# Four gate tiles ahead of the convolution's fourth tile in a two-layer hybrid diffusion step

## The chip, the cores and the metric

The kernel runs on one core of one Trainium2 chip. The metric is the device time of one execution in microseconds (us), from which a median over runs is taken. PE stands for TensorE, DVE for VectorE, ACT for ScalarE, POOL for GpSimd and SP for SyncE, whose queue issues the transfers. A line number such as L1300 is a line of the kernel before; in the changed kernel the same code stands two lines lower from L576 on.

## The reference

A step of a small diffusion backbone runs two layers over 128 context tokens and 1,024 latent tokens of width 1,024. All arithmetic is float32. In each layer a token's row is normalised and modulated to h, one projection of h gives the inputs of three branches, and the branches are gated, projected and added to the residual:

```python
(shift, scale, gate) = SiLU(cond) @ W_ada + b_ada
h = RMSNorm(x) * (1 + scale) + shift
[A | B | C] = split(h @ W_in)
y_A = B_g * conv3(C_g * x_A) * SiLU(g_A)
y_B = neighbourhood_attention(q, k, v) * SiLU(g_B)
y_C = RMSNorm(bidirectional_gated_linear_attention(q, k, v)) * SiLU(g_C)
merged = sum_b sigmoid(h @ W_gate + b_gate)_b * (y_b @ W_branch[b])
x = x + gate * (merged @ W_out)
```

Branch A is a convolution of three taps along the tokens. Branch B lets every latent token attend to a window of the 16 x 64 grid and to all cached context keys. Branch C carries a 64 x 128 state per head through the sequence in both directions, chunk by chunk.

## The kernel before, in words

**Precision and tiles.** Each float32 operand of the large products is held as a high and a low part, and a product is three matmuls (high by high, high by low, low by high). The 1,152 tokens stand in three chunks of 384. A feature tile is 128 columns of a weight matrix: `load_w` (L186) lets SP fetch it (512 KB into the tile `wraw`), ACT make the high part `whi` (L182) and POOL the low part `wlo` (L183). `mode_a` (L223) multiplies it by one chunk: 8 x 3 = 24 matmuls of 128 x 384 into one bank `ps`, of which there are two in turn. Whatever reads a `ps` bank must be done before PE may fill it again, two chunks later.

**The main work of a layer** is written out in `layer` (L527). After the projections of values, keys and queries come four convolution tiles (`conv`, L1275), four tiles of SiLU for the attention (`silus`, L1326), sixteen gate tiles (`gates`, L589), four gated tiles of the linear attention (`gated`, L1317) and five more gate tiles. They all multiply h, so on PE they look alike; they differ in what empties the banks:

- `conv` makes four products per chunk and tile. In its first half ACT copies `xa` (L1285) and DVE multiplies `u` (L1288). Over the whole row of 1,154 columns DVE then forms the three taps `cv` (L1291 to L1293). In the second half DVE multiplies by the taps into `y1` (L1300; the profile calls the tile `y`), and ACT, DVE and POOL form the SiLU `th` (L1307 to L1309).
- `gates` makes one product per chunk. ACT alone empties the bank (L596), and SP stores `gt` to `gd` (L597).
- `silus` empties the bank with ACT (L1332) and DVE (L1333).

**The side work** is woven into PE's order by the class `Pace`: each main matmul adds its planned microseconds to a credit, and when that is full, one step of the side work is written into PE's order. The side work is first the linear attention (`gla`) and then the neighbourhood attention (`attention`). The places where it goes therefore depend on how many main matmuls have been written, not on which tile they belong to. In `gla` the recurrence of states (L1160) is a chain of DVE operations that is written after the last chunk's matmuls:

```python
nS = g1.tile([128, GH, DV], F32, name="gs", tag=("qk1", "la")[i % 2])
...
for h in range(GH):
    dve.scalar_tensor_tensor(nS[r, h], S[r, h], dec[r, c + 1, h:h + 1], u[:, h], op0=ALU.mult, op1=ALU.add)
```

It has 56 such operations in each layer. In `attention` every item (a head, a row group and a column block) has a stage with scores (DVE L933, ACT L934, DVE L938 and L939), one with transposes (ACT L962, DVE L963) and one that multiplies by the values.

**A third strand** is `adaln` (L281), the modulation for the gate and the next layer. It is a list of generators called `extras`; `silus`, `gates` and `gated` call `extra()` after each chunk, and every other call makes one step of it. A step fetches 512 KB of `w_ada` into a `wraw` tile and multiplies it on ACT (L294), DVE (L299) and POOL (L296, L297).

**What sets the order.** PE's instructions keep the order in which the program writes them. The order on DVE, ACT, POOL and SP is chosen by the scheduler that builds the program, so operations can move ahead of others that were written earlier. Each engine then runs its own list strictly in order.

Of the kernel before, what the change touches and what calls it, by code (L numbers as in the profile page):

```python
# [112 lines left out]
def hybrid_step(ctx: ExitStack, tc: tile.TileContext, io: dict):  # L113
# [4 lines left out]
    def pool(name, bufs=2, side="left", **kw):  # L118
        return tc.tile_pool(name=name, bufs=bufs, side=side, reuse_waits="tile", **kw)
# [66 lines left out]
    def load_w(pieces, nk, lo_engine=gps):  # L186
        return split_w(*raw_w(pieces, nk), lo_engine)

    def wview(w, l, c0, n):
        return w[l].rearrange("(k p) c -> p k c", p=128)[:, :, c0:c0 + n]  # L190
# [336 lines left out]
    def layer(l):  # L527
        d = Scratch(l)
        win = lambda c0, n: wview(io["w_in"], l, c0, n)
        fw_stack = ExitStack()  # L530
        fw = fw_stack.enter_context(pool(f"fw_{l}"))
        s1_stack = ExitStack()
        with ExitStack() as s0_stack:
            projections(l, d, win, s1_stack, s0_stack, fw)
        main_us = 47.0 + (16 + 4 + 4 + 21) * 3 * 24 * 0.163 + (19.0 if l + 1 < DEPTH else 8.0)
        extras = []

        turn = [0]

        def extra():  # L540
            turn[0] += 1
            while extras and turn[0] % 2:
                try:
                    next(extras[0])
                    return
                except StopIteration:
                    extras.pop(0)

        def side():
            yield from gla(l, d)  # L550
            left = main0 + main_us - pace.main
            pace.rate = NH * 23 / max(left - 20.0, 40.0)
            yield from attention(l, d)

        main0 = pace.main

        def begin():
            s1_stack.close()
            pace.start(side(), RATE_G)

        pace.defer(14.0, begin)
        with pool(f"vp_{l}") as vp:
            values(l, d, win, vp)
        cv_stack = ExitStack()
        cvp = cv_stack.enter_context(pool(f"cv_{l}"))
        extras = [adaln(l, 2, cvp, wraw)]
        if l + 1 < DEPTH:
            extras += [adaln(l + 1, 0, cvp, wraw), adaln(l + 1, 1, cvp, wraw)]
        for m in range(4):
            conv(l, m, win, fw, cvp, d.yd[0])  # L570
        for m in range(4):
            silus(l, m, win, fw, GN, d.yd[1], extra)
        gates(l, range(0, 16), fw, "y1", 2, d.gd, extra)
        for m in range(4):
            gated(l, m, win, fw, GG, d.ogd, keep(d.yd[2]), extra)
        gates(l, range(16, 21), fw, "y1", 2, d.gd, extra)  # L576
        while extras:
            turn[0] = 0
            extra()
        pace.drain()  # L580
        cv_stack.close()
        fw_stack.close()
        with pool(f"yp_{l}", 3) as yp:
            first = branch_input(l, d, 0, yp, yp)
            gates(l, range(21, 24), yp, "gl", 3, d.gd)
            rest = branches(l, d, yp, first)
        output(l, *rest)

    def gates(l, tiles, tp, tag, bufs, gd, extra=lambda: None):  # L589

        for m in tiles:
            wg = load_w([wview(io["w_gate"], l, m * 128, 128)], KD)
            for c in range(NCH):
                ps = mode_a(wg, H, KD, c)
                gt = tp.tile([128, CH], F32, name="gt", tag=tag, bufs=bufs)
                act.activation(gt, ps, ACTF.Tanh, scale=0.5, bias=C["b_gate"][:, l, m:m + 1])  # L596
                sp.dma_start(gd[m * 128:(m + 1) * 128, c * CH:(c + 1) * CH], gt)  # L597
                extra()
# [23 lines left out]
    def values(l, d, win, vp):  # L622

        for u in range(2):
            mode_b([win(VN + u * 256, 256)], H, split_values(l, d, vp, u))
        for j in range(4):
            a = d.vd[TP + KCS[j]:TP + KCS[j] + 1, :]
            src = bass.AP(tensor=a.tensor, offset=a.offset, ap=[[128 * BW, 16], [1, 64 * BW]])
            sp.dma_start(d.vw[j], src)
# [641 lines left out]
    def segs(c):  # L1271

        return ((0, 128, 0), (128, 256, 130)) if c == 0 else ((0, 384, CH * c + 2),)

    def conv(l, m, win, fw, cvp, yd):  # L1275
        wx = load_w([win(XA + m * 128, 128)], KD)
        wc = load_w([win(CA + m * 128, 128)], KD)
        u = cvp.tile([128, T + 4], F32, name="u", tag="u", bufs=1)
        gps.memset(u[:, 0:1], 0.0)
        gps.memset(u[:, 129:131], 0.0)  # L1280
        gps.memset(u[:, T + 3:T + 4], 0.0)
        for c in range(NCH):
            ps = mode_a(wx, H, KD, c)
            xa = cvp.tile([128, CH], F32, name="xa", tag="xa")
            act.copy(xa, ps)  # L1285
            ps = mode_a(wc, H, KD, c)
            for o, n, p in segs(c):
                dve.tensor_tensor(u[:, p + 1:p + 1 + n], ps[:, o:o + n], xa[:, o:o + n], op=ALU.mult)  # L1288
        cv = cvp.tile([128, T + 2], F32, name="cv", tag="cv", bufs=1)
        w = lambda i: C["conv_w"][:, l, m, i:i + 1]  # L1290
        dve.tensor_scalar(cv, u[:, 0:T + 2], w(0), None, op0=ALU.mult)  # L1291
        dve.scalar_tensor_tensor(cv, u[:, 1:T + 3], w(1), cv, op0=ALU.mult, op1=ALU.add)
        dve.scalar_tensor_tensor(cv, u[:, 2:T + 4], w(2), cv, op0=ALU.mult, op1=ALU.add)  # L1293
        wb = load_w([win(BA + m * 128, 128)], KD)
        wg = load_w([win(GA + m * 128, 128)], KD)
        for c in range(NCH):
            ps = mode_a(wb, H, KD, c)
            y1 = fw.tile([128, CH], F32, name="y1", tag="y1")
            for o, n, p in segs(c):
                dve.tensor_tensor(y1[:, o:o + n], ps[:, o:o + n], cv[:, p:p + n], op=ALU.mult)  # L1300
            ps = mode_a(wg, H, KD, c)
            keep(yd)(c, m, silu2_times(ps, y1, fw, "th"))
# [9 lines left out]
    def keep(yd):  # L1312
        def f(c, m, y):
            sp.dma_start(yd[m * 128:(m + 1) * 128, c * CH:(c + 1) * CH], y)
        return f

    def gated(l, m, win, fw, c0, od, out, extra):  # L1317
        wg = load_w([win(c0 + m * 128, 128)], KD)
        for c in range(NCH):
            y1 = fw.tile([128, CH], F32, name="y1", tag="y1")  # L1320
            sp.dma_start(y1, od[m * 128:(m + 1) * 128, c * CH:(c + 1) * CH])
            ps = mode_a(wg, H, KD, c)
            out(c, m, silu2_times(ps, y1, fw, "th"))
            extra()

    def silus(l, m, win, fw, c0, zd, extra):  # L1326

        wg = load_w([win(c0 + m * 128, 128)], KD)
        for c in range(NCH):
            ps = mode_a(wg, H, KD, c)  # L1330
            th = fw.tile([128, CH], F32, name="th", tag="th")
            act.activation(th, ps, ACTF.Tanh, scale=0.5)  # L1332
            dve.scalar_tensor_tensor(th, th, 1.0, ps, op0=ALU.add, op1=ALU.mult)  # L1333
            keep(zd)(c, m, th)
            extra()

    def branch_input(l, d, b, yp, home):

        Y = {}
        for c in range(NCH):  # L1340
            if home is yp:
                Y[c] = [yp.tile([128, 4, CH], F32R, name=f"y{x}", tag=f"y{x}", bufs=3) for x in "hl"]
            else:
                Y[c] = [hp.tile([128, KD, CH], F32R, name=f"h{x}", tag=f"h{x}") for x in ("hi", "lo")]
            yh, yl = Y[c]
            at = lambda t, k: t[k * 128:(k + 1) * 128, c * CH:(c + 1) * CH]
            for k in range(4):
                ys = yp.tile([128, CH], F32, name="ys", tag="ys", bufs=4)
                sp.dma_start(ys, at(d.yd[b], k))
                if b == 1:  # L1350
                    on = yp.tile([128, CH], F32, name="on", tag="ys", bufs=4)
                    sp.dma_start(on, at(d.ond, k))
                    gps.tensor_tensor(ys, ys, on, op=ALU.mult)
                act.copy(yh[:, k], ys)
                dve.tensor_tensor(yl[:, k], ys, yh[:, k].bitcast(F32), op=ALU.subtract)
        return Y
# [102 lines left out]
    with tc.manual_schedule(engines={mybir.EngineType.PE}):  # L1459
        for l in range(DEPTH):  # L1460
            layer(l)
# [93 lines left out]
```

## Time and profile before

| | |
|---|---|
| median of 3 runs | 2787.06 us (2779.57 to 2788.96) |
| profiled execution, its own time | 2782.12 us |
| its span | 2780.3 us |
| PE busy | 2705.2 us, 97% of the span |
| DVE busy | 1189.2 us, 43% |
| ACT busy | 936.9 us, 34% |
| POOL busy | 1042.1 us, 37% |
| mean granted clock of PE | 0.996 |

The span runs from the first instruction's start to the last one's end; the execution's own time is 1.8 us longer. PE's matmuls overlap, so its busy share tells when it had something to do and not that it ran at its peak. A wait in the trace is a stretch in which an engine had nothing to run, with the instruction of another engine (the releaser) that ended it. Layer 0's main work with its side work fills about 350 to 1120 us of the span, layer 1's about 1720 to 2490 us.

### The profile page before, as it was taken

The numbers are of one execution on the slowest core, as the hardware profiler recorded it, in microseconds if no ns is written. First come the engines' busy times: TensorE is split into PE (matmuls) and PEld (weight loads), VectorE is DVE, ScalarE is ACT, GpSimd is POOL, SyncE is SP. The second block draws the span as 40 slices with busy tenths as digits, with TensorE's granted clock in tenths as the row PEclk, the third lists the DMA queues.
The fourth block names the chain that finished last, engine by engine and source line by source line (L and its number), as shares of the span: only waits on it lengthen the run. The fifth ranks groups of instructions, "written<-read, shape, count | busy, mean of one in ns | idle before, by whom it ended". The sixth has DMA issues, their size and how long they took to land. (4 is left out here: it accounts for less than half of the span.)

```text
span 2780.3 us, 47973 instructions
## 1 busy us (share of the span) xinstructions
PE 2705.2 (97%) x18548; PEld 2655.0 (95%) x18548; DVE 1189.2 (43%) x2400; ACT 936.9 (34%) x1802; POOL 1042.1 (37%) x884
## 2 busy tenths in 40 slices
PE   6999999999999999999989999999999999999999
PEld 4999999999999999999989999989999999999999
DVE  5344335545444443335173452364453334432441
ACT  5243322233444433312242442222244343342120
POOL 0343233463574431167343332333532112212852
PEclk9999999999999999999999999999999999999999
DMA  7444672365565653565234447623655455435651
GB/s 235 120 130 129 196 238 71 110 183 142 168 181 154 169 157 94 177 185 181 74 122 119 127 127 226 211 68 124 164 147 154 134 146 154 137 111 180 176 181 69
DMA packets 455740, 415.26 MB, mean 149 GB/s; under 512 B 84740, under 2 KB 422028, under 8 KB 455248
## 3 DMA queue, kind: packets, MB, share of 16 engines
q1 hardware_dynamic: 455504, 412.13, 50.1%
q8 instruction: 146, 2.39, 0.4%
q14 instruction: 90, 0.74, 0.1%
HBM read 292.04 MB, written 136.74 MB: 154 GB/s over the span
## 5 line engine op out<-in xcount | busy, mean ns | idle before, releaser
L131 PE MATMUL ps<-hhi,whi 128*128 128x384 f32 x2368 | 807.3, 341 | 17.6 <-DVE y L1300 6.7
L131 PE MATMUL ps<-hhi,wlo 128*128 128x384 f32 x2368 | 804.9, 340 | 0.3
L131 PE MATMUL ps<-hlo,whi 128*128 128x384 f32 x2368 | 805.1, 340 | 0.0
L183 POOL TENSOR_TENSOR wlo<-wraw,whi 128x1024 fp32r<-128x1024 f32 (+2 forms) x172 | 369.0, 2145 | 803.1 <-ACT whi L182 739.9
L131 PE MATMUL ps<-whi,hhi 128*128 128x256 f32 (+1 forms) x1984 | 567.1, 286 | 5.8 <-DVE ro L616 2.4
L131 PE MATMUL ps<-wlo,hhi 128*128 128x256 f32 (+1 forms) x1984 | 567.0, 286 | 2.1 <-DVE wlo L183 2.1
L131 PE MATMUL ps<-whi,hlo 128*128 128x256 f32 (+1 forms) x1984 | 566.6, 286 | 0.0
L131 PEld LDWEIGHTS ps<-hhi,whi 128*128 128x128 f32 x2368 | 447.0, 189 | 23.7 <-DVE y L1300 6.5
L131 PEld LDWEIGHTS ps<-hlo,whi 128*128 128x128 f32 x2368 | 447.1, 189 | 2.1 <-issue 1.4
L131 PEld LDWEIGHTS ps<-hhi,wlo 128*128 128x128 f32 x2368 | 446.8, 189 | 1.8 <-issue 0.9
L131 PEld LDWEIGHTS ps<-whi,hhi 128*128 128x128 f32 x1984 | 379.9, 192 | 9.3 <-PE ps L131 3.1
L131 PEld LDWEIGHTS ps<-wlo,hhi 128*128 128x128 f32 x1984 | 379.9, 191 | 4.3 <-DVE wlo L183 3.3
L131 PEld LDWEIGHTS ps<-whi,hlo 128*128 128x128 f32 x1984 | 380.1, 192 | 0.6 <-issue 0.3
L182 ACT CAST whi<-wraw 128x1024 fp32r<-128x1024 f32 (+1 forms) x200 | 189.4, 948 | 372.0 <-PE ps L131 164.2
L963 DVE TENSOR_TENSOR ptl<-psb,pth 128x640 fp32r<-128x640 f32 x128 | 105.3, 823 | 189.2 <-ACT pth L962 188.9
L934 ACT ACTIVATE prob<-prob,mn 128x640 f32<-128x640 f32 x128 | 106.2, 830 | 191.8 <-DVE mn L933 191.4
L933 DVE CUSTOM_DVE_ANT_0 prob<-psb,bt 128x640 f32<-128x640 f32 x128 | 105.3, 822 | 100.0 <-PE psb L131 85.7
L296 POOL TENSOR_SCALAR adapr<-wraw,scond 128x256 f32<-128x256 f32 x112 | 110.0, 982 | 93.7 <-DMA wraw<-in_w_ada 44.5
L153 POOL TENSOR_TENSOR rs_y<-rs_a,mhalf 128x12 f32<-128x12 f32 (+2 forms) x42 | 78.3, 1864 | 140.5 <-DVE rs_a L151 135.4
L962 ACT CAST pth<-psb 128x640 fp32r<-128x640 f32 x128 | 88.5, 692 | 114.5 <-PE psb L135 113.8
L1402 POOL TENSOR_TENSOR mx<-mx,gl 128x384 f32<-128x384 f32 x96 | 108.5, 1141 | 23.8 <-DVE gl L1401 22.9
L596 ACT ACTIVATE gt<-ps,b_gate 128x384 f32<-128x384 f32 x144 | 83.3, 579 | 87.7 <-PE ps L131 63.0
(248 smaller groups left out, 3903.9 us busy)
## 6 DMA issues: line engine op xcount, KB each, us to landing
wraw<-in_w_in SPq DMA_DIRECT2D x88, 512.0 KB, 4.6
gd<-gt SPq DMA_DIRECT2D x144, 192.0 KB, 2.1
gl<-gd SPq DMA_DIRECT2D x144, 192.0 KB, 2.6
wraw<-in_w_gate SPq DMA_DIRECT2D x48, 512.0 KB, 4.3
wraw<-in_w_ada SPq DMA_DIRECT2D x32, 512.0 KB, 4.2
qt<-qld SPq DMA_DIRECT2D x128, 128.0 KB, 3.1
vt<-vw SPq DMA_DIRECT2D x64, 256.0 KB, 3.4
wraw<-in_w_branch SPq DMA_DIRECT2D x48, 256.0 KB, 3.4
```

What stands on the lines that cost most here:

```text
L131: pe.matmul(out, lhsT, rhs, **kw)
L153: gps.tensor_tensor(y, a, mhalf[:, 0:n], op=ALU.pow)
L182: act.copy(hi[:, 0:n], raw[:, 0:n])
L183: lo_engine.tensor_tensor(lo[:, 0:n], raw[:, 0:n], hi[:, 0:n].bitcast(F32), op=ALU.subtract)
L296: gps.tensor_scalar(pr, rv[:, kk], w, None, op0=ALU.mult)
L596: act.activation(gt, ps, ACTF.Tanh, scale=0.5, bias=C["b_gate"][:, l, m:m + 1])
L933: dve.tensor_tensor_reduce(p[:, 0:n], ps[:, lo:lo + n], bias, 1.0, 3e38, ALU.add, ALU.min, mn)
L934: act.activation(p[:, 0:n], p[:, 0:n], ACTF.Exp, bias=mn, scale=-1.0, accum_out=sums)
L962: act.copy(to[0], src)
L963: dve.tensor_tensor(to[1], src, to[0].bitcast(F32), op=ALU.subtract)
L1402: gps.tensor_tensor(mv[c][:, m, :], mv[c][:, m, :], gt, op=ALU.add)
```

## The change

Four of the first sixteen gate tiles are made between the third and the fourth tile of the convolution, without calls of `extra()`. The other twelve stay where the sixteen were. Nothing is computed that was not computed before, and nothing is left out. Both layers have the change.

```diff
-        for m in range(4):
+        for m in range(3):
             conv(l, m, win, fw, cvp, d.yd[0])
+        gates(l, range(0, 4), fw, "y1", 2, d.gd)
+        conv(l, 3, win, fw, cvp, d.yd[0])
         for m in range(4):
             silus(l, m, win, fw, GN, d.yd[1], extra)
-        gates(l, range(0, 16), fw, "y1", 2, d.gd, extra)
+        gates(l, range(4, 16), fw, "y1", 2, d.gd, extra)
```

DVE in layer 0 around the recurrence, in the kernel before: `gs` is the recurrence, `y` and `th` are the second half of a convolution tile, and the last two rows begin the next tile.

```order
L1120 TENSOR_TENSOR su<-psm,al 128x512
L1160 SCALAR_TENSOR_TENSOR gs<-gs,dec,su 64x128 x16
L1300 TENSOR_TENSOR y_5305<-ps,cv 128x384
L1160 SCALAR_TENSOR_TENSOR gs<-gs,dec,su 64x128 x17
L1308 SCALAR_TENSOR_TENSOR th<-th,ps 128x384
L1160 SCALAR_TENSOR_TENSOR gs<-gs,dec,su 64x128 x10
L1300 TENSOR_TENSOR y_5490<-ps,cv 128x384
L1160 SCALAR_TENSOR_TENSOR gs<-gs,dec,su 64x128
L1308 SCALAR_TENSOR_TENSOR th<-th,ps 128x384
L1288 TENSOR_TENSOR u<-ps,xa 128x128
L1288 TENSOR_TENSOR u<-ps,xa 128x256
```

In the changed kernel these rows read the same (with L1122, L1162, L1302, L1310 and L1290 for the lines). The first row of DVE's list that differs comes after the third convolution tile is done, in layer 0 and again in layer 1.

ACT in layer 0 from the third convolution tile's last SiLU on, before: `ott` is the output of the linear attention, `xa` is the convolution's, `adaacc` the modulation's.

```order
L1307 ACTIVATE th<-ps 128x384
L1213 ACTIVATE ott<-psm,gla_norm_w 128x384 x2
L1285 COPY xa<-ps 128x384
L1213 ACTIVATE ott<-psm,gla_norm_w 128x384
L294 ACTIVATE adaacc<-wraw,scond 128x256 x2
L1213 ACTIVATE ott<-psm,gla_norm_w 128x384 x3
L1285 COPY xa<-ps 128x384
```

And now:

```order
L1309 ACTIVATE th<-ps 128x384
L1215 ACTIVATE ott<-psm,gla_norm_w 128x384 x2
L598 ACTIVATE gt<-ps,b_gate 128x384
L1215 ACTIVATE ott<-psm,gla_norm_w 128x384 x2
L598 ACTIVATE gt<-ps,b_gate 128x384
L1215 ACTIVATE ott<-psm,gla_norm_w 128x384 x2
L182 CAST whi<-wraw 128x1024
L598 ACTIVATE gt<-ps,b_gate 128x384
```

The gates' twelve `gt` take the place of the fourth tile's `xa` beside the linear attention's output, and the modulation's first step moves behind them.

DVE in layer 0 in the middle of the fourth convolution tile, before: `u` of the last chunk, the taps, and what the second half begins with.

```order
L1288 TENSOR_TENSOR u<-ps,xa 128x384
L1291 TENSOR_SCALAR cv<-u,conv_w 128x1154
L1292 SCALAR_TENSOR_TENSOR cv<-u,conv_w,cv 128x1154
L1293 SCALAR_TENSOR_TENSOR cv<-u,conv_w,cv 128x1154
L1300 TENSOR_TENSOR y_6516<-ps,cv 128x128
```

And now, from the row behind the same `u` on:

```order
L935 ISA prob,mn<-psb,bt 128x640
L935 ISA mn 128x1
L1293 TENSOR_SCALAR cv<-u,conv_w 128x1154
L299 SCALAR_TENSOR_TENSOR adaacc<-wraw,scond,adaacc 128x256
L1294 SCALAR_TENSOR_TENSOR cv<-u,conv_w,cv 128x1154
L940 RECIPROCAL rsum<-sums 128x1
L299 SCALAR_TENSOR_TENSOR adaacc<-wraw,scond,adaacc 128x256
L1295 SCALAR_TENSOR_TENSOR cv<-u,conv_w,cv 128x1154
L965 TENSOR_TENSOR ptl<-psb,pth 128x5x128
L941 TENSOR_SCALAR prob<-prob,rsum 128x640
L299 SCALAR_TENSOR_TENSOR adaacc<-wraw,scond,adaacc 128x256
L1302 TENSOR_TENSOR y_7120<-ps,cv 128x128
```

The taps, which stood in one block, are now mixed with the neighbourhood attention (`prob`, `mn`, `rsum`, `ptl`) and with the modulation (`adaacc`).

## Rows read from the trace of the kernel before

**Rows 1.** The page's busy times by engine, over the whole span.

```profile
PE 2705.2 (97%) x18548; PEld 2655.0 (95%) x18548; DVE 1189.2 (43%) x2400; ACT 936.9 (34%) x1802; POOL 1042.1 (37%) x884
```

**Rows 2.** PE's waits, whole span: waiter, releaser: us in total, times, longest.

```profile
PE ps L131 <- DVE y L1300: 6.7, 6, 2.9
...
PE ps L131 <- DVE th L1308: 5.9, 2, 2.9
...
PE psb L135 <- DVE ptl L963: 4.0, 2, 3.5
PE ps L131 <- DVE th L1333: 3.4, 1, 3.4
```

**Rows 3.** DVE's timeline, layer 0: start, us, operation, count, [idle before, releaser].

```profile
474.83 6.95 DVE L1160 SCALAR_TENSOR_TENSOR gs<-gs,dec,su 64x128 f32<-64x128 f32 x16
...
489.65 6.71 DVE L1160 SCALAR_TENSOR_TENSOR gs<-gs,dec,su 64x128 f32<-64x128 f32 x10
...
505.73 0.62 DVE L1288 TENSOR_TENSOR u<-ps,xa 128x128 f32<-128x128 f32 x2 [7.33 <-PE ps L131]
```

**Rows 4.** PE's waits from 480 to 500 us.

```profile
PE ps L131 <- DVE th L1308: 2.9, 1, 2.9
PE ps L131 <- DVE y L1300: 1.8, 2, 1.3
```

**Rows 5.** PE's waits on `y` from 1860 to 1880 us, the same place in layer 1.

```profile
PE ps L131 <- DVE y L1300: 2.9, 1, 2.9
```

**Rows 6.** Windows: stretch, length, busy PE, PEld, DVE, ACT, POOL (count), clock, DMA, GB/s.

```profile
482.00:498.00 16.00, 11.47 (x53) 10.83 (x54) 15.14 (x32) 8.27 (x22) 7.40 (x6) 0.89 0.13 38
...
1980.00:2006.00 26.00, 21.66 (x124) 20.73 (x123) 13.89 (x30) 10.03 (x21) 18.12 (x17) 0.94 0.63 164
```

**Rows 7.** PE's waits from 560 to 620 us, the fourth convolution tile.

```profile
PE ps L131 <- DVE y L1300: 0.8, 1, 0.8
```

**Rows 8.** DVE's timeline in the middle of the fourth tile, layer 0.

```profile
584.04 0.56 DVE L1288 TENSOR_TENSOR u<-ps,xa 128x384 f32<-128x384 f32 x1 [3.69 <-PE ps L131]
584.64 2.51 DVE L1291 TENSOR_SCALAR cv<-u,conv_w 128x1154 f32<-128x1154 f32 x1
587.18 3.43 DVE L1292 SCALAR_TENSOR_TENSOR cv<-u,conv_w,cv 128x1154 f32<-128x1154 f32 x1
590.65 1.50 DVE L1293 SCALAR_TENSOR_TENSOR cv<-u,conv_w,cv 128x1154 f32<-128x1154 f32 x1
592.25 0.62 DVE L1300 TENSOR_TENSOR y<-ps,cv 128x128 f32<-128x128 f32 x2
```

**Rows 9.** The taps over the whole span, by tile: duration min/median/max in ns.

```profile
L1291 DVE TENSOR_SCALAR cv<-u,conv_w x8: 822/962/2508, 387.5 to 1959.0; 128x1154 f32<-128x1154 f32 x8
L1292 DVE SCALAR_TENSOR_TENSOR cv<-u,conv_w,cv x8: 1420/2968/3432, 388.3 to 1961.5; 128x1154 f32<-128x1154 f32 x8
L1293 DVE SCALAR_TENSOR_TENSOR cv<-u,conv_w,cv x8: 1421/1502/3443, 392.4 to 1965.0; 128x1154 f32<-128x1154 f32 x8
```

**Rows 10.** A long main stretch of PE in the chain that ended last: start, us, count.

```profile
1906.57 19.48 PE ps L131 x111
```

**Rows 11.** DVE's timeline: first and last of layer 0's twelve SiLU chunks.

```profile
617.67 0.55 DVE L1333 SCALAR_TENSOR_TENSOR th<-th,ps 128x384 f32<-128x384 f32 x1
...
680.07 0.54 DVE L1333 SCALAR_TENSOR_TENSOR th<-th,ps 128x384 f32<-128x384 f32 x1
```

**Rows 12.** Groups by line, shapes apart: count, us busy, mean ns, idle before, releasers.

```profile
L933 DVE CUSTOM_DVE_ANT_0 prob<-psb,bt 128x640 f32<-128x640 f32 x128 | 105.3, 822 | 100.0 <-PE psb L131 85.7 <-DMA bt<-t2d 9.1 <-DMA ond<-ot 2.1
...
L299 DVE SCALAR_TENSOR_TENSOR adaacc<-wraw,scond,adaacc 128x256 f32<-128x256 f32 x112 | 66.4, 593 | 54.3 <-ACT adaacc L294 27.7 <-DMA wraw<-in_w_ada 25.0
```

**Rows 13.** DVE's timeline in layer 1, ahead of the wait of 3.4 us.

```profile
1999.92 0.48 DVE L299 SCALAR_TENSOR_TENSOR adaacc<-wraw,scond,adaacc 128x256 f32<-128x256 f32 x1 [6.14 <-DMA wraw<-in_w_ada]
```

**Rows 14.** POOL's timeline beside the taps of rows 8.

```profile
583.10 2.92 POOL L846 MEMSET bt<- 128x1664 f32 x2
...
586.49 2.90 POOL L183 TENSOR_TENSOR wlo<-wraw,whi 128x1024 fp32r<-128x1024 f32 x1
```

## The prediction

> **What bounds the kernel.** The page's busy times come first: PE has work for 97% of the span, and no other engine for more than 43% [rows 1]. So the time is PE's list run in order plus its waits, and a change that leaves the matmuls alone can only move waits. PE's waits come next, and those on the three main strands are few [rows 2]: six on the convolution's `y`, two on its `th`, two on attention's `ptl`, one on the SiLU's `th`. A wait is also what the clock follows: in the stretch with the waits of the recurrence the mean clock was 0.89, and in layer 1's stretch with the 3.4 us wait it was 0.94 [rows 6]. So (1 - 0.89) x 16 us = 1.8 us of full-speed work was lost in the one and (1 - 0.94) x 26 us = 1.6 us in the other, beside the waits themselves.
>
> **Where the recurrence is.** The recurrence blocks DVE from 474.8 us on in pieces of nearly 7 us, the last of which ends at 489.65 + 6.71 = 496.4 us [rows 3]. DVE is busy for 15.14 of 16 us there [rows 6], and PE waits behind it for `th` and `y`: 2.9 + 1.8 = 4.7 us in layer 0 [rows 4], and 2.9 + 2.9 = 5.8 us in layer 1, of which `y` has its row there [rows 5] and `th` is the second of the two waits that no other place has [rows 2]. Those `y` and `th` belong to the second half of a convolution tile. Which tile? The next `u` comes at 505.73 us [rows 3], and the fourth tile's last `u` at 584.04 us [rows 8]. In one tile the first and the last `u` are about four products apart, 4 x 24 matmuls of 19.48 / 111 = 0.1755 us [rows 10], or 17 us plus side work. So the `u` at 505.73 opens the third tile, and the recurrence runs in the second. The order says the same: the recurrence stands ahead of that `u` before and now, and DVE's list differs only after the third tile. The four gates come after the recurrence is over, since `Pace` places the side work by main matmuls written, and these are the same up to there.
>
> **The change part by part.**
>
> *The recurrence's waits stay.* 4.7 and 5.8 us, with the clock they cost: 0 us of change.
>
> *The matmuls* are the same in number and shape: 4 x 3 x 24 go earlier, none is added: 0 us. Four weight fetches of 512 KB move with them, into the slots in which the fourth tile's four fetches stood, and twelve stores of `gt` come earlier on SP's queue. Their cover is the gates' own pace: a gate tile asks PE for 72 x 0.1755 = 12.6 us and one weight tile, as a convolution's weight does. I cost both at nothing. Were the cover gone, PE would wait for a weight tile, which no row of rows 2 shows.
>
> *The gates' stretch.* Where the fourth tile stood, beside the linear attention's output, PE now meets banks that ACT alone empties. The one wait of the old tile there, 0.8 us on `y` in layer 0 [rows 7], goes, and so does its twin in layer 1: six waits on `y` make 6.7 us [rows 2], of which rows 4, 5 and 7 name 1.8 + 2.9 + 0.8, so that 1.2 us are left for the two others, of which I put 0.7 here. That is -1.5 us.
>
> *The fourth tile's new place.* It now runs beside the neighbourhood attention at full rate. What is late next is `y`: from the last `u` to the first `y` DVE must do its list while PE has two more products of 24. Before, DVE took 592.25 + 0.62 - 584.04 = 8.8 us [rows 8] and PE's 48 matmuls alone 48 x 0.1755 = 8.4 us, which fits the wait of 0.8 us. Now PE's share is longer, because attention's matmuls stand between: eleven SiLU chunks beside attention took 680.07 - 617.67 = 62.4 us [rows 11], 5.7 us a chunk, so two products give DVE 11.3 us. And DVE's list is longer. By the order there are, beside the taps, one `u` (0.56), one `mn` with its score pass (0.82), three modulation products (0.59 each) [rows 8, 12], a reciprocal, `ptl` and a scaling, which have no row here and which I put at 0.2, 0.8 and 0.6 us (an estimate, by the score pass over the same 640 columns), and `y` (0.62). That is 0.56 + 0.82 + 1.77 + 1.6 + 0.62 = 5.4 us. The three taps are between 0.82 + 1.42 + 1.42 = 3.7 us, each at its shortest [rows 9], and 2.51 + 3.43 + 1.50 = 7.4 us [rows 8]. DVE's sum is 9.1 to 12.8 us against 11.3 us: a wait of 0 to 1.5 us, and I take the middle, 0.7 us, since rows 9 have medians between the ends. For two layers that is +1.4 us.
>
> *The modulation* starts about 50 us later and is squeezed, 75 calls of `extra()` for 87. It carries the larger old waits: in layer 1 DVE stood 6.14 us at a modulation product until its `w_ada` had landed [rows 13], and PE then waited 3.4 us for the `th` queued behind; the 3.5 us on `ptl` [rows 2] is the same pattern in layer 0. With 16 blocks of modulation in two layers, two made such a wait. The change aligns every later block anew, and no row says which will be late. Bounds: both vanish, -(3.5 + 3.4 + 2 x 1.6 of clock) = -10.1 us; or two more come, +10.1 us. I take 0, two of sixteen again.
>
> *Sum:* -1.5 + 1.4 + 0 = -0.1 us on the profiled execution's 2782.1 us, thus 2782. That execution lies 4.9 us below the median of the three runs, and inside their spread of 9.4 us. I forecast against the median and a little towards the profiled execution: **2786 us**. About 0.3%, or 8.4 us, is what a measurement of this kernel can tell from no change.
>
> **What rule and row say of the taps.** POOL's 2.90 us `wlo` and the fills before it lie over the taps [rows 14], and the second tap took 3.43 us where 1.42 is its least [rows 8, 9]. It ended at 590.6 us, 1.2 us after `wlo`'s end at 589.39: it waited and then ran. The Trainium skill ("SBUF — State Buffer", section "Who interferes with whom") says that a DVE instruction with two operands in SBUF and a GpSimd instruction that reads SBUF take one shared port in turn, and that the later one is blocked completely. The trace agrees. By that rule moving the taps among POOL's modulation products and splits could block every one of them, which speaks against this change; it is the second rival below.
>
> **The rivals.**
>
> 1. *DVE's late modulation moves into the tile (slower).* Place: a modulation product between the taps and the first `y`, in either layer. DVE would stop there for a landing as in rows 13, 6.1 us; the slack is 11.3 - 9.1 = 2.2 us at best, so PE waits 3.9 us and loses 1.6 us of clock, 5.5 us a layer, 11 us in all: 2797. It decides once `w_ada` lands more than 2.2 us after DVE gets there. For it: the order has three such products there. Against: 14 of 16 blocks made no wait of 3 us or more, and these are fetched early. Chance 0.14.
> 2. *Each tap waits for POOL.* Three taps behind a `wlo` of 2.9 us: 3.7 + 3 x 2.9 = 12.4 us, DVE 5.4 + 12.4 = 17.8 us, PE waits 6.5 us a layer, 13 us: 2799. Against: only four splits fall on a whole tile, so three within this window is rare, and POOL's fill of `bt` [rows 14] is by now over. Chance 0.05.
> 3. *The squeezed modulation falls clear (faster).* Both old late blocks find their data landed, and the taps are short: -1.5 - 10.1 = -11.6 us, 2774. For it: `silus` now follows two early blocks. Chance 0.11.
> 4. *The gates do cover the recurrence.* -4.7 - 5.8 - 1.8 = -12.3 us, 2774. Against it stand rows 3 and the unchanged order. Chance 0.03.
>
> **How the numbers follow.** The forecast has 0.67. Its own range is -6 to +6 us: one late block more or less (3.4 + 1.6 = 5 us) and the run-to-run spread. The range 2774 to 2799 reaches the ends of the rivals and leaves out their far sides, under 0.2. Faster: rivals 3 and 4 without the part that a measurement would not tell, plus the forecast's lower edge, 0.15. Slower: rivals 1 and 2 and the upper edge, 0.18. Within 0.3%: 0.67.
>
> **What would show it.** Right: PE waits on `th` and `y` around 482 to 497 us exactly as before, and again in layer 1; no wait on `y` from 560 to 610 us; a wait of at most 1.5 us at the first `y` of the fourth tile, now near 640 us; about two waits over 3 us behind modulation products. Wrong: no waits around 482 to 497 us, or a wait of over 4 us in the new fourth tile, or a total that moves while PE's waits do not.

## The result, and the profile after

The changed kernel takes **2798.2 us** (median of 6 runs, 2793.64 to 2806.45); beside it the kernel before took 2783.86 us. The ratio is 1.0056, 95% interval 1.0041 to 1.007: some 15 us slower, where no change was forecast. The profiled execution took 2806.45 us and is the longest of the six, 8 us above the median; so the single waits and differences read from its trace below add up to more than the 15 us. Its span is 2804.7 us and its mean granted clock 0.987, where the kernel before had 0.996; half of that difference lies in the first 40 us (0.66 against 1.00), ahead of the change.

The page's busy times after: as many instructions on every engine as in [rows 1], and 8 us more of PE, which fits its having run longer at the lower clock level (behind the wait at 607 us below its matmuls start 0.32 us apart, and 0.17 us apart 3 us later).

```profile
PE 2713.3 (97%) x18548; PEld 2662.4 (95%) x18548; DVE 1185.1 (42%) x2400; ACT 937.7 (33%) x1802; POOL 1041.1 (37%) x884
```

PE's waits over the whole span (waiter, releaser: us in total, times, longest), to be held against [rows 2]:

```profile
PE ps L131 <- ACT gt L598: 8.7, 5, 3.1
...
PE ps L131 <- DVE th L1310: 6.8, 3, 3.0
PE ps L131 <- DVE y L1302: 6.7, 4, 2.9
...
PE psm L131 <- DVE ptl L965: 6.2, 4, 2.5
...
PE psb L135 <- DVE ptl L965: 5.5, 4, 2.9
```

`y` has the same 6.7 us as before in four waits instead of six, and the 3.4 us on the SiLU's `th` has gone. New are 8.7 us on the gates' `gt`, and the waits on `ptl` have grown from 4.0 us to 11.7 us. The waits of the recurrence, 480 to 506 us, are those of [rows 4] but for the last, 2.9 us where it was 1.3, as it was in layer 1 before [rows 5]; among the runs below it takes either value where nothing differs up to there:

```profile
PE ps L131 <- DVE y L1302: 3.3, 2, 2.9
PE ps L131 <- DVE th L1310: 2.8, 1, 2.8
```

Where did the time go? Both traces have 18548 matmuls, so the starts of the matmuls of the same number can be compared along the program. The table takes the difference from matmul 1500 on; what lies ahead of it (5.9 us here, from -0.9 to 4.5 us in the runs below) is start-up, which the change doesn't touch and which differs from one execution to the next.

| matmul | its start before, us | changed minus before | where |
|---|---|---|---|
| 4000 | 561 | +2.1 | ahead of the change, 1.4 of it the wait just named |
| 4500 | 644 | +6.0 | gates and fourth tile, layer 0 |
| 5000 | 730 | +2.8 | the SiLU tiles gave 3.2 back |
| 6000 | 890 | +15.3 | gate tiles beside attention: **+12.5** |
| 12500 | 1815 | +14.8 | |
| 13500 | 1984 | +17.6 | gates, layer 1 |
| 14000 | 2069 | +15.3 | given back |
| 18500 | 2769 | +18.5 | 3.2 more, 1.6 of them a `gt` wait at 2215 us |

So three things stand beside each other: a loss at the moved gates, a gain soon behind it, and the largest loss 150 us further on, in gate tiles that the change didn't move.

**The moved gates.** SP's queue in layer 0 (start, us, operation, count):

```profile
590.75 8.35 SPq L863 DMA_DIRECT2D bt<-t2d  x16
...
603.17 0.92 SPq L599 DMA_DIRECT2D gd<-gt  x2
```

and ACT's timeline beside it:

```profile
592.70 0.57 ACT L598 ACTIVATE gt<-ps,b_gate 128x384 f32<-128x384 f32 x1
596.13 0.58 ACT L598 ACTIVATE gt<-ps,b_gate 128x384 f32<-128x384 f32 x1 [2.85 <-issue]
602.29 0.30 ACT L880 CAST vc<-vraw 128x128 fp32r<-128x128 f32 x1 [5.58 <-DMA vraw<-in_cache_v]
...
606.83 1.07 ACT L598 ACTIVATE gt<-ps,b_gate 128x384 f32<-128x384 f32 x2 [1.56 <-DMA gd<-gt]
```

The `gt` of 592.70 us was ready to be stored at 593.3, but its store is issued at 603.17: attention's first head has just put 16 loads of `bt` on SP, 8.35 us, and more loads behind them. `gt` has two buffers, so the third stands until the first store is done, and PE meets a full bank: a wait of 3.10 us that ends at 607.47 us, with the clock at its lower level for 3.4 us behind it (0.88 in the mean of 598 to 612 us, below). Layer 1 has the twin, 3.04 us.

**The fourth tile** waits for `ptl`, 1.6 us, not for `y`. **Given back:** the 3.5 us on `ptl` at 701 us [rows 2] has gone. The windows show both; first the changed kernel, columns as in [rows 6]:

```profile
598.00:612.00 14.00, 10.90 (x55) 10.58 (x54) 0.00 (x0) 2.41 (x4) 2.80 (x2) 0.88 0.73 198
660.00:672.00 12.00, 10.41 (x58) 10.16 (x57) 10.39 (x15) 3.60 (x8) 9.87 (x7) 0.86 0.63 149
700.00:716.00 16.00, 16.00 (x103) 15.93 (x102) 7.29 (x15) 6.03 (x12) 2.40 (x1) 1.00 0.47 144
...
895.00:912.00 17.00, 14.09 (x73) 13.77 (x73) 8.82 (x15) 7.20 (x13) 13.06 (x12) 0.80 0.49 144
```

then the kernel before, in the last two of these places (the changed kernel makes the matmuls of 690 to 706 us from 704.7 to 715.3 us, and the last windows of both lists end about matmul 6005):

```profile
690.00:706.00 16.00, 12.50 (x69) 12.14 (x68) 8.69 (x16) 7.90 (x15) 9.01 (x7) 0.89 0.44 139
...
874.00:891.00 17.00, 17.00 (x109) 16.93 (x108) 6.49 (x15) 7.37 (x14) 2.41 (x1) 1.00 0.62 176
```

From 874 to 891 us PE never stopped before and POOL did one instruction; now the 17 us up to the same matmul, 895 to 912 us, have twelve on POOL, 73 matmuls for 109, and the clock at 0.80. Ten of POOL's twelve are the modulation's, which had none in that stretch before, and two are splits of weights.

**The gate tiles beside attention.** PE's waits from 760 to 1060 us, changed:

```profile
PE psb L135 <- DVE ptl L965: 5.0, 3, 2.9
PE psm L131 <- DVE ptl L965: 2.5, 1, 2.5
PE ps L131 <- DVE th L1310: 1.0, 1, 1.0
```

and before:

```profile
PE psm L131 <- ACT pth L962: 1.4, 2, 1.0
PE ps L131 <- ACT gt L596: 1.0, 1, 1.0
PE psb L135 <- DVE ptl L963: 0.5, 1, 0.5
```

In the two largest, 2.53 us at 838 and 2.91 us at 901 us, `ptl` stands behind a modulation product on DVE. At 838 us DVE stood at that product for 6.47 us until its `w_ada` had landed; the load was issued at 832.95 us, when POOL's product that read the buffer before had ended (832.00 + 0.92):

```profile
836.75 0.93 DVE L299 SCALAR_TENSOR_TENSOR adaacc<-wraw,scond,adaacc 128x256 f32<-128x256 f32 x1 [6.47 <-DMA wraw<-in_w_ada]
```

At 901 us ACT stood at `whi`, and `op` and `pth` behind it:

```profile
895.37 1.05 ACT L182 CAST whi<-wraw 128x1024 fp32r<-128x1024 f32 x1 [4.38 <-DMA wraw<-in_w_gate]
896.45 0.27 ACT L971 ACTIVATE op<-psm 64x128 f32<-64x128 f32 x1
896.75 0.70 ACT L964 CAST pth<-psb 128x640 fp32r<-128x640 f32 x1
```

DVE, which had waited for `op`, then made three modulation products, and `ptl` began at 900.57 us, 3.1 us after `pth` was done:

```profile
896.96 3.69 DVE L299 SCALAR_TENSOR_TENSOR adaacc<-wraw,scond,adaacc 128x256 f32<-128x256 f32 x3
```

Three theories follow for the experiments. **A**: the stores of `gt` behind the loads of `bt`. **B**: DVE in the fourth tile beside attention's start. **D**: the modulation runs 12 groups of 24 matmuls later, and its lateness costs; in three forms, D1 (DVE waits for `w_ada`), D2 (the products' own time on DVE), D3 (neither; the modulation shares the three `wraw` buffers and the queues of SP, ACT and POOL with the weights).

### The profile page after: what moved, and what is told of

It reads as the page before. It is cut to its first block, busy times and chain, and to the rows that moved or that the text cites. A ratio compares the mean times of both kernels' runs of the same rounds, so it can differ in the third digit from the quotient of the medians.

```text
span 2804.7 us, 47958 instructions
## 1 busy us (share of the span) xinstructions
PE 2713.3 (97%) x18548; PEld 2662.4 (95%) x18548; DVE 1185.1 (42%) x2400; ACT 937.7 (33%) x1802; POOL 1041.1 (37%) x884
```

## The experiments

Eighteen kernels. The kernel before ran beside each, with medians of 2782.48 to 2783.54 us; ratios are to it, are taken from all its runs there, and can differ from the ratio of two medians by up to 0.1%. Where an experiment has several kernels, the forecasts stand in the order of the results.

**Four buffers for `gt`** (changed kernel):

```
-        gates(l, range(0, 4), fw, "y1", 2, d.gd)
+        gates(l, range(0, 4), fw, ("y1", "th"), 2, d.gd)
...
-                gt = tp.tile([128, CH], F32, name="gt", tag=tag, bufs=bufs)
+                gt = tp.tile([128, CH], F32, name="gt", tag=tag if isinstance(tag, str) else tag[(3 * m + c) % 2], bufs=bufs)
```

> The changed kernel, but the moved gates write their output alternately into the tiles of y and of th, so that four of them can wait for their store instead of two. Theory A (the third gate output waits for a buffer because the stores stand behind 16 bias loads on SP): the wait on gt near 607 us, 3.1 us, and its twin in layer 1, 3.0 us, go, and with them 1.6 us of clock each, so about 9 us less than the changed kernel: 2789 us. Rival (ACT's list is held by the cast of the context values, whose load is late): the wait stays at over 2 us in both layers and the time at 2798 us.

Measured 2798.09 us, ratio 1.006 (1.0047 to 1.0073). The waits on `gt` went in both layers, and the time stayed. PE's waits from 590 to 700 us in this run:

```profile
PE psm L131 <- DVE ptl L965: 4.0, 1, 4.0
PE ps L131 <- DVE u L1290: 1.7, 1, 1.7
```

What A took away came back in the fourth tile, 5.7 us where there had been 2.0. A is a wait, but not the price.

**The modulation back at its old matmuls** (changed kernel, `extra()` called 12 times in the fourth tile):

```
-        conv(l, 3, win, fw, cvp, d.yd[0])
+        conv(l, 3, win, fw, cvp, d.yd[0], extra)
...
+            extra()
+            extra()
```

> The changed kernel, but the fourth tile calls extra() twelve times, so that the modulation stands at the same main matmuls as before the change. Theory D (in layer 0 the later modulation meets attention at worse places, some 14 us between 770 and 1040 us): the waits on ptl between 770 and 910 us, 6.9 us and 5 us of clock, go, and the time falls to 2786 to 2790 us. Rival (the fourth tile's new place alone makes them): they stay, and the time is 2798 us or more.

Measured 2795.37 us, ratio 1.0041 (1.0028 to 1.0054). Only 3 or 4 us came back, so the time is neither theory's. In the trace the waits on `ptl` from 760 to 1060 us did fall, from 7.5 to 2.8 us, and the loss between matmuls 5000 and 6000 from 12.5 to 5.2 us; a `pth` wait of 1.8 us and a `gt` wait of 1.3 us stand there in their place.

**The four gate tiles behind the fourth tile:**

```
+        conv(l, 3, win, fw, cvp, d.yd[0])
         gates(l, range(0, 4), fw, "y1", 2, d.gd)
-        conv(l, 3, win, fw, cvp, d.yd[0])
```

> All four convolution tiles in their old place, then the four gates without extra(), then the rest: the modulation is as late as in the changed kernel, the convolution as early as before. Theory D: the waits of layer 0's gates stay, and the time is 2792 to 2798 us. If the fourth tile beside attention or the stores behind the bias loads make most of the loss, the time is that of the kernel before, 2780 to 2786 us.

Measured 2792.29 us, ratio 1.0037 (1.0025 to 1.005). No wait on `gt` at 600 us, no new wait in the fourth tile, yet `ptl` waited 9.0 us between 560 and 1060 us: A and B are gone, and 10 of the 15 us of loss are still there.

**The four gate tiles inside the second tile**, where the recurrence runs:

```
+        if m == 1:
+            gates(l, range(0, 4), fw, "y1", 2, gd)
         wb = load_w([win(BA + m * 128, 128)], KD)
```

> The four gates stand between the two halves of the second tile, where the recurrence runs; the modulation is as late as in the changed kernel. If the recurrence's waits are DVE holding up the second half, as rows 3 to 5 show, PE's waits on th and y there, 4.7 and 6.3 us, go in both layers, and ACT alone empties the banks meanwhile: 11 us less than e3. With theory D that is 2782 to 2787 us, without it 2770 to 2776 us. Rival: the gates' stores or ACT's part in the recurrence hold the banks up instead, and nothing is won.

Measured 2786.59 us, ratio 1.0015 (1.0006 to 1.0025), the best of those that compute everything in another order. PE's waits from 470 to 500 us are now

```profile
PE ps L131 <- ACT gt L596: 2.6, 2, 1.9
```

for 4.7 us before [rows 4]: gates do cover the recurrence when they stand there, but not wholly, since ACT multiplies the recurrence's states (`su`, L1165) and `gt` queues behind that. The loss of D stays (`ptl` waits 7.5 us from 760 to 1060 us).

**The modulation late, and nothing else** (kernel before):

```
-            silus(l, m, win, fw, GN, d.yd[1], extra)
+            silus(l, m, win, fw, GN, d.yd[1], lambda: None)
```

> The kernel before, its order of weight tiles untouched; only the four silu tiles lose their 12 calls of the modulation, so that it begins 12 groups of matmuls later, as in the changed kernel. Theory D (the modulation's lateness by itself costs time, as its products on DVE then meet attention's): slower than before by 5 to 11 us, nearly all in layer 0, with ptl waits of 1 to 3 us between 770 and 960 us; of that a gain of up to 5 may come back at 620 to 700 us, where DVE has fewer products. Rival (the lateness is harmless, and what the four earlier runs lost between 770 and 1040 us came from attention's own start or from where the gates are): within 2 us of before, and no ptl wait over 1 us between 770 and 960.

Measured 2795.73 us, ratio 1.0038 (1.0022 to 1.0053). No weight tile moved, and PE's waits from 760 to 1060 us are much like the changed kernel's:

```profile
PE psb L135 <- DVE ptl L963: 3.3, 3, 2.3
PE psm L131 <- DVE ptl L963: 2.4, 1, 2.4
PE psm L131 <- ACT pth L962: 1.9, 2, 1.4
```

By matmuls, as in the table above, this run is 0.8 us ahead at 5000, 8.7 us behind at 6000 and 11.5 us at the end. So in the old order of the weights the lateness by itself costs 6 to 15 us: D is shown there, though not which of its three forms.

**Undoing the lateness in other orders.** Gates in the second tile with the 12 calls back in the fourth:

> The four gate tiles between the two halves of the second convolution tile, beside the recurrence, and the modulation's 12 first calls in the fourth convolution tile, which here stands at the matmuls where the first silu tiles stood before. Theory D: the run with the gates in tile 2 (+3.8 us to before) loses its 7 to 8 us of layer 0 and keeps the 2.4 and 2.3 us that it gains at the recurrences: 2777 to 2781, faster than both kernels. Rival (the modulation in the fourth tile, whose DVE work is the heaviest, costs what its lateness cost): 2785 to 2792.

2791.82 us, ratio 1.003 (1.0015 to 1.0046). Changed kernel with four buffers and the 12 calls back:

> The changed kernel with both mends at once: gt in four buffers, and the modulation's 12 first calls back at their old matmuls, in the fourth tile. If the two losses are separate and add up: no gt wait near 605 and 1993 us, no ptl waits at 770 to 900, and 2783 to 2789. If DVE in the fourth tile beside attention's start is what both were given back to: ptl or u waits of 4 us and more in the fourth tile in both layers, and 2793 to 2800.

2791.77 us, ratio 1.0027 (1.0011 to 1.0042). Silu tiles and first four gate tiles changed over, the 12 calls in those gates:

> The kernel before with the first four gate tiles and the four silu tiles changed over; conv tiles and the modulation's calls stand at the matmuls where they stood before. Differs from the run with the gates behind the fourth tile (+9.5 us to before) by the modulation's 12 calls alone. Theory D: that run's loss falls by 7 us or more: within 3 us of before or faster. Rival (lateness harmless): within 2 us of that run, 2790 to 2794.

2792.44 us, ratio 1.0025 (1.0012 to 1.0038). All three miss what D promised: with the calls at their old matmuls but another weight tile beside them, the waits return elsewhere (`ptl` 2.5 us at 762, `gt` 2.6 us at 824 us in the first; `ptl` 2.5 us at 767 in the second; `mn` 5.5 us at 614, `pth` 4.2 us at 700 us in the third, where at 614 us ACT had stood 8.5 us at the modulation's first multiplication until `w_ada` had landed). So lateness isn't the whole of it: these three orders, in which the modulation stands where it stood but beside other weight tiles, cost 7 to 8 us. How much of that is the moved tiles by themselves, these three don't show.

**Loads of `w_ada` one step ahead of their products**, in four kernels:

```
-                rv = raw_tile()[:, 0:1024].rearrange("p (k c) -> p k c", k=4)
-                sp.dma_start(rv, wview(io["w_ada"], l, c0, 256)[:, 4 * kh:4 * kh + 4, :])
+                rv = nxt.pop()
+                if (nb, kh) != (3, 1):
+                    nxt.append(fetch(nb + kh, 1 - kh))
```

> The changed kernel; only each load of w_ada is issued one step of the modulation earlier than the products that read it (in the changed kernel the load and its products are issued in one step, so DVE stands 4 to 6 us in front of a product while attention's ptl is queued behind it, as at 830 to 837 us). Theory D1 (the modulation costs time because its products hold DVE until the load lands): the ptl waits at 778, 838 and perhaps 901 us go, no wait of DVE on a w_ada load over 1 us is left, and the time falls by 5 to 9 us from 2798 to 2789 to 2793. Rival D2 (it is the products' own DVE time, stretched beside POOL, as 3.69 us for three at 897 us): within 3 us of 2798.

> The kernel before with the loads of w_ada one step ahead and nothing else. D1: DVE's six waits on a w_ada load (25 us together, mostly beside nothing that matters in this kernel) go; 2778 to 2783, the same or up to 5 us faster. D2: within 2 us of before.

> The gate tiles between the halves of the second convolution tile, beside the recurrence, with the modulation late and its loads one step ahead. D1: of the run without it (+3.8 us to before) the 7.6 us of layer 0 go: 2777 to 2782, a little faster than before. D2: within 2 us of that run, 2785 to 2789.

> The kernel before with the modulation 12 groups late, no gates moved (that run: +12.5 us, ptl waits of 2.44 us at 831 and 2.31 at 894), and its loads one step ahead. D1: the waits at 831 us and about go, +2 to +6 us to before. D2: +10 us or more, as without it.

Measured 2820.27, 2814.72, 2808.84 and 2810.55 us, ratios 1.0133, 1.0114, 1.0092 and 1.0101, each within 0.002 either way. The changed kernel's wait for `ptl` at 838 us went, and these came between 700 and 1060 us:

```profile
PE ps L131 <- ACT whi L182: 9.7, 2, 4.9
PE ps L131 <- POOL wlo L183: 4.4, 4, 1.8
```

A load issued a step earlier holds one of the three `wraw` buffers a step longer, and the weights' fetches come late. A miss for D1's forecast, but no clean test of D1: it took away one wait and made a larger one, and in the changed kernel DVE still stood at a `w_ada` load five times, 12.0 us in all and up to 3.7 us. It pointed at the buffers.

**DVE's products without their waits, then without the products**, each in the changed kernel and in the one before:

```
-                            dve.scalar_tensor_tensor(acc[:, s], rv[:, kk], w, acc[:, s], op0=ALU.mult, op1=ALU.add)
+                            dve.scalar_tensor_tensor(own.rearrange("p (a b) -> p a b", a=4), con, w, con, op0=ALU.mult, op1=ALU.add)
```

(in the second pair the line is `pass`).

> The changed kernel, with DVE's 112 products of the modulation kept in number and nearly in size (128x248) and place, but reading a constant and writing a tile of their own, so that they wait for no load of w_ada, no ACT and no POOL; the output lacks their share of the modulation's sums. D1 (the waits for the load cost): no ptl wait at 838 us, 5 to 8 us below the changed kernel, 2790 to 2793. D2 (the products' own time) or D3: within 3 us of 2798.

> The kernel before with the same replacement; leaves out the same share. D1: the change's cost inside this pair falls from 15 us to 6 to 9 us. D2, D3: it stays at 11 us or more. The kernel itself: 2776 to 2783 (its own waits on w_ada, 25 us of DVE, stood before little that PE waited for).

> The changed kernel without DVE's 112 products of the modulation at all (leaves out their share of the sums; loads, ACT's and POOL's share stay). D1 or D2: 2783 to 2790, no ptl wait over 1 us between 770 and 960 us; D1 alone: equal to the run with products of a constant within 3 us. D3: 2794 to 2800.

> The kernel before without DVE's products of the modulation (leaves out the same share): 2774 to 2782. The change's cost inside this second pair: D1 or D2 4 to 8 us (what the gates in front of the fourth tile cost by gt's stores and the fourth tile), D3 11 us or more.

Measured 2794.93 (1.0038, 1.0026 to 1.0049) against 2784.53 us (0.9997, 0.9985 to 1.0009), and 2794.55 (1.003, 1.0017 to 1.0043) against 2782.29 us (0.999, 0.9978 to 1.0003). Inside either pair the change still costs 0.4%, of 0.56%. By these ratios D1 and D2 together are about a quarter of it; the intervals allow anything from nothing to some two thirds. The traces, of one execution each, put them higher in the largest loss: between matmuls 5000 and 6000 the change costs 4.5 us inside the first pair and 3.8 us inside the second, for 12.5 us. In the changed kernel without products, PE still waits 2.22 us for `ptl` at 837 us, and the way back is plain. POOL's timeline:

```profile
829.38 0.93 POOL L296 TENSOR_SCALAR adapr<-wraw,scond 128x256 f32<-128x256 f32 x1
```

SP's queue:

```profile
830.33 0.39 SPq L173 DMA_DIRECT2D wraw<-in_w_gate  x1
```

ACT's timeline:

```profile
834.43 1.05 ACT L182 CAST whi<-wraw 128x1024 fp32r<-128x1024 f32 x1 [4.86 <-DMA wraw<-in_w_gate]
835.38 0.69 ACT L964 CAST pth<-psb 128x640 fp32r<-128x640 f32 x1
```

and DVE's:

```profile
836.10 0.82 DVE L965 TENSOR_TENSOR ptl<-psb,pth 128x640 fp32r<-128x640 f32 x1 [7.90 <-ACT pth L964]
```

POOL's product ends at 829.38 + 0.93 = 830.31; 0.02 us later SP issues the fetch of the next `w_gate` into the buffer; it lands 4.1 us after; ACT has stood 4.86 us at the cast, with attention's `pth` behind it; `ptl` follows `pth`, and PE follows `ptl`.

**The products of POOL and DVE kept in number, reading constants**, so that they neither hold a `wraw` buffer nor wait for `w_ada`:

```
-                            gps.tensor_scalar(pr, rv[:, kk], w, None, op0=ALU.mult)
-                            gps.tensor_tensor(acc[:, s], acc[:, s], pr, op=ALU.add)
+                            gps.tensor_scalar(pr.rearrange("p (a b) -> p a b", a=2), ident.unsqueeze(1).to_broadcast([128, 2, 128]), w, None, op0=ALU.mult)
+                            gps.tensor_tensor(pr, acc[:, s], pr, op=ALU.add)
```

> The changed kernel with the modulation's products on DVE and on POOL kept in number, but reading constants (DVE 248 columns, POOL 256), so that they neither wait for the loads of w_ada nor hold their buffers; only ACT's 32 multiplications still read them. Leaves out most of the modulation's sums. D3 by the buffers (POOL holds a wraw buffer, the fetch of w_gate comes late, ACT stands in front of whi with pth behind): ACT's waits in front of whi between 570 and 1060 us fall from 54 to under 25 us, the ptl waits at 770 to 960 us are under 1 us, 2785 to 2790. Rival (the work itself, on POOL or DVE, or the places of the gates): 2793 to 2798.

> The kernel before with the same replacement. D3 by the buffers: 2776 to 2782, and the change's cost inside this pair 4 to 8 us (the gt stores and the fourth tile, nearly all of it before 700 us and near 2000 us). Rival: the cost inside the pair stays at 10 us or more.

Measured **2778.06** us (0.9981, 0.997 to 0.9992) and **2776.72** us (0.9974, 0.9963 to 0.9985). The change's cost falls from 15 us to 1 or 2 us, with intervals that overlap; 4 to 8 us had been expected, and 2785 to 2790 us for the changed one. PE's waits from 570 to 1060 us in the changed one with constants are all of these:

```profile
PE ps L131 <- ACT gt L600: 4.0, 2, 3.0
PE psm L131 <- DVE ptl L967: 0.3, 1, 0.3
```

So where POOL and DVE don't read the modulation's loads, the waits on `ptl` are gone and the moved tiles cost little. What ACT waited for in front of its casts from 570 to 1060 us (the group of the cast `whi` by line: releaser, us, times) was in the kernel before

```profile
DMA wraw<-in_w_gate: 38.4, 12
```

in the changed one

```profile
DMA wraw<-in_w_gate: 39.6, 12
DMA wraw<-in_w_in: 18.7, 4
```

in the changed one with constants

```profile
DMA wraw<-in_w_gate: 2.9, 1
```

and in the one before with constants

```profile
DMA wraw<-in_w_gate: 15.4, 3
```

The sum alone is no price: the kernel before with DVE's products of a constant has 53.7 us of such waits and takes no longer than the kernel before. Place decides, that is, whether a `ptl` or `gt` that PE needs next stands behind the cast.

## Why the prediction was wrong

- **The recurrence's waits stay: right.** 6.1 us in layer 0 and 6.4 us in layer 1, for 4.7 and 5.8 us forecast; in layer 1 the kernel before had 6.3 us, as one more wait on `y`, 0.5 us, lies just ahead of the window of rows 5. Putting the same gates into the second tile showed what covering it is worth: 2.4 us by matmul 4000, not the 4.7 us that the fourth rival reckoned with for this layer.
- **"Four weight fetches and twelve stores … I cost both at nothing": mis-sized.** The cover named, the gates' pace on PE, was the wrong one; the stores stand on SP behind 16 loads of `bt`, and with two buffers that is a 3.1 us wait a layer and half-speed matmuls behind it. But taken away it brought nothing, and in the pair with constants it is still there (2.98 us) while the change costs 1 or 2 us. The waits near 701 and 2001 us that went gave as much back; why they went, no run shows. So its net is small, and the forecast's zero was nearly right for a reason that it didn't have.
- **The old tile's 0.8 us on `y` goes, and its twin in layer 1: right.** Of the six waits on `y` the four of the recurrence are left.
- **The fourth tile: right in size, not in kind.** DVE's list from the last `u` to the first `y` took 668.74 + 0.61 - 657.10 = 12.3 us, inside the 9.1 to 12.8 forecast, and there was no wait on `y`. PE waited 1.6 us for attention's `ptl`, which stands in front of that `y` on DVE. One product took 2.54 us there beside POOL's split. POOL's timeline:

```profile
661.07 3.58 POOL L183 TENSOR_TENSOR wlo<-wraw,whi 128x1024 fp32r<-128x1024 f32 x1
```

and DVE's, from the last `u` to the first `y`:

```profile
657.10 0.56 DVE L1290 TENSOR_TENSOR u<-ps,xa 128x384 f32<-128x384 f32 x1 [0.48 <-PE ps L131]
...
662.40 2.54 DVE L299 SCALAR_TENSOR_TENSOR adaacc<-wraw,scond,adaacc 128x256 f32<-128x256 f32 x1
...
666.67 0.81 DVE L965 TENSOR_TENSOR ptl<-psb,pth 128x640 fp32r<-128x640 f32 x1
...
668.74 0.61 DVE L1302 TENSOR_TENSOR y<-ps,cv 128x128 f32<-128x128 f32 x2
```

It ends 0.3 us after the split, where such a product alone takes 0.48 us [rows 13]. The rule that the Trainium skill gives ("SBUF — State Buffer", section "Who interferes with whom") agrees with it again, to 0.2 us. By it the second rival was to hit all three taps; two of them took their least, 0.82 and 1.42 us.
- **"The modulation … I take 0, two of sixteen again": this is the step that failed.** The bounds were -10.1 and +10.1 us; moved alone it cost 6 to 15 us. The forecast let two late blocks fall at random. In the runs the old order was a good one, and the first eight kernels of the experiments, with the modulation late or in place beside other tiles, cost 4 to 17 us by their ratios. The way is also wider than the forecast's rows 13. It took DVE in front of `w_ada` for the only door; by the ratios of the pairs the larger part needs POOL's products too, and the chain traced at 830 us goes through them, the shared buffers, SP's fetch and ACT's cast, of which the forecast has no term. That second door stood open in the kernel before: the 3.5 us on `ptl` at 701 us, which the forecast called "the same pattern" as rows 13, isn't it. ACT stood at a cast whose `w_gate` was late, with `pth` behind it, and DVE was idle until `pth` came. ACT's timeline before:

```profile
698.54 1.04 ACT L182 CAST whi<-wraw 128x1024 fp32r<-128x1024 f32 x1 [2.74 <-DMA wraw<-in_w_gate]
699.49 0.69 ACT L962 CAST pth<-psb 128x640 fp32r<-128x640 f32 x1
```

and DVE's:

```profile
700.21 0.82 DVE L963 TENSOR_TENSOR ptl<-psb,pth 128x640 fp32r<-128x640 f32 x1 [1.73 <-ACT pth L962]
```

- **The first rival** (slower by a late modulation) had the sign, and 2797 us against 2798 measured; the near number is luck, as its place was the fourth tile and its door DVE. It was given 0.14; the position of the moved work against attention deserved more, since the forecast itself said that every later block is aligned anew.
- **What would show it**: the forecast named about two waits over 3 us behind modulation products as right. There is none over 3 us now, but four of 1.46 to 2.91 us on `ptl` between 660 and 905 us, and the clock's lower level beside three of them. Of its signs of being wrong none came true: none watched the gate tiles behind the moved ones.

What stays open: the pair with constants took from POOL and DVE both the hold on the buffers and the wait for `w_ada`; DVE's part is about a quarter by the ratios of the pairs before, POOL's holding and waiting weren't tried apart. ACT's multiplications of the modulation read `w_ada` in every kernel. A fourth `wraw` buffer wasn't tried. A version that computes everything and beats the kernel before wasn't found.

## What to carry to other kernels

A piece of work that is called "in between" moves whenever what carries it moves: list what each moved call fetches, which buffers that takes from whom, and which engine stands in order behind the fetch. A wait that is found and named isn't yet the price: take it away and see whether the time falls. Where two streams share a small ring of buffers, the slowest reader can set the other stream's fetch, and an engine that casts in program order passes that lateness on to work that has nothing to do with it.

## What the runs showed that was not expected

Issuing a load a step earlier cost 15 to 32 us here, in each of the four kernels against its own form without it. And POOL and DVE stand 69.5 us at `w_ada` in the kernel before (44.5 and 25.0 us, whole span); taking that away, together with the hold on the buffers, brought only some 6 us: 2783 us against 2777. The start-up, up to about 160 us, differed by up to 6.8 us between the traces (from -0.9 to +5.9 us against the kernel before), although all kernels have the same order of instructions there.
